# Two gate tiles turned from plain projections into a seven-product pair, and weight loads sorted later, in a planned f32 attention block

## Chip, cores and metric

One core of one Trainium2 chip. The metric is the device time of one execution in microseconds (us), the median of three runs. The kernel is one launch; nothing is computed on the host but constants.

## What is computed

One pre-norm layer on `x` of 512 tokens by 1024 channels, all in f32. One combined projection feeds two attention branches, their SiLU gates and two sigmoid gates. Cut to what matters here:

```
h = rmsnorm(x, norm_g)
(q_lat, c_kv, k_rope, z_a, q_b, k_b, v_b, z_b,
 q_idx, k_idx, w_idx, gate_a, gate_b) = split(h @ w_in)
y_a = mla_attention(...) * silu(z_a)             # 512 wide, dense, chunk-causal
y_b = dsa_attention(..., topk=128) * silu(z_b)   # 512 wide, top-k keys by an indexer
merged = sigmoid(gate_a) * (y_a @ w_o_a) + sigmoid(gate_b) * (y_b @ w_o_b)
out = rmsnorm(x + merged @ w_out, final_g)
```

`gate_a` and `gate_b` are 1024 wide, that is eight tiles of 128 channels each: ga0 to ga7 and gb0 to gb7. `z_b` has four tiles, zb0 to zb3.

## The kernel before, in words

**Arithmetic.** TensorE works in a rounded f32 format, so every operand is split into a high and a low part. The high part is a cast on ScalarE (ACT), the low part a subtraction (`lo_part`, L399, by `tt`, L346) on VectorE (DVE) or GpSimd (POOL). One f32 product is then three matmuls (`mm3`): high by high, high by low, low by high.

**Order.** No loop of the program is the order of the work. Python generators yield steps, and `Flow` (L140 to L258) is a list scheduler that runs at build time: at each turn it takes the step with the smallest key, which is the modelled start time, plus a margin that TensorE (PE) and the DMA queue keep behind other engines (`SETTLE`), plus a small weight of the thread's priority, plus `t.nudge`, a random number below 0.01 us drawn once for each thread from `random.Random(DRAW)`. What comes out is one fixed in-order stream for each engine. All weight loads sit on the DMA queue of SyncE (SP), in order with the other transfers there.

**Weight jobs.** `QUEUE` (L2078) lists the weight tiles. `fetcher` (L953) takes them in that order, gets one of four raw buffers (512 KB each) and issues the load; `splitter` (L967) makes high and low parts; `multiplier` (L980) yields the matmuls, which PE takes between the steps of the attention. A lower-case name is a plain projection (`proj`, L988): 8 blocks of the contraction by 3 matmuls of 128x512, 24 in all, into one PSUM bank. Upper-case names go in twos (`proj2`, L1038): two tiles are one 2x2 block product done by seven products of blocks (`seven`, L1102) instead of eight. Each of the seven is 4 blocks by 3 matmuls of 128x256, 84 for two tiles. For this the weights are summed and subtracted first (`prep`, L1053), seven instead of four pairs of parts are cast and subtracted, and the seven results are put together by two copies on ACT and five 128x256 additions from PSUM on DVE into the slots called `s_pair`. The inputs of the products are sums of blocks of h, `s_hs`; when the last pair has been multiplied, `pair_done` (L1141) gives the `s_hs` slots back and sets "pairs".

**What hangs on "pairs".** `y_gate` (L1690) multiplies the attention result by its SiLU gate, waits for "pairs" (L1698) since its slots `s_ys` are those of `s_hs`, and splits the product: a cast on ACT and one 128x512 scalar_tensor_tensor (STT, L357) on DVE for each of the eight tiles. The first output projection (`branch_out`, L1749; 4 blocks by 3 matmuls of 128x512 with the weights `w_o`) reads `s_ys`. The eight tiles of gate A were moved out to DRAM early (`bias_scratch` serves as that place); when the last projection of all has been emitted ("projections"), `fetch_gates` (L1286) issues their eight loads of 256 KB on SP.

**The tail of the queue.** `ou` takes a load of `w_out` weights, which are only split at that time and multiplied at the end. Before the change the tail is `GB4 GB5 ou zb3 gb6 ou gb7 ou`: one pair, then three plain projections.

**Held loads.** `PASSED` (L2083) holds back the loads of jobs 7 to 10: their DMA is emitted only after 2, 2, 2 and 6 more transfers have been emitted on SP (`hold`, `passed`, L439 to L449). `passed_by` (L1100) does the like for one low part of the values of branch B, which is emitted behind the next addition of a pair.

Of the kernel before, what the change touches and what calls it, by code (L numbers as in the profile page):

```python
# [80 lines left out]
class Step:  # L81
# [58 lines left out]
class Flow:  # L140
# [57 lines left out]
    def run(self, stop=None):  # L198
        while self.threads:
# [15 lines left out]
            for t in self.threads:  # L215
                if isinstance(t.req, Step):
                    for i, (eng, dur, emit) in enumerate(t.req.options):
                        s = self.start(t.req, eng)
                        key = ((self.settled(t.req, eng, s) if eng in SETTLE and s < math.inf else s) + BIAS * t.prio + t.nudge, t.prio)
                        if len(t.req.options) > 1:  # L220
                            fin = s + dur + {"POOL": self.pbias if t.req.pbias is None else t.req.pbias, "ACT": t.req.abias}.get(eng, 0.0)
                            cand = (fin, s, eng, dur, emit, key)
                        else:
                            cand = (0.0, s, eng, dur, emit, key)
                        if i == 0 or cand[0] < mine[0]:
                            mine = cand
                    if best is None or mine[5] < best[1][5]:
                        best = (t, mine)
# [34 lines left out]
NUDGE = 0.01  # L263
DRAW = 53
PSQUARE = -50
# [5 lines left out]
def tile_block(ctx: ExitStack, tc: tile.TileContext, a: dict, out: bass.AP, bias_dram: bass.AP):  # L271
# [166 lines left out]

    held = []  # L439

    def hold(n, emit):

        return lambda: held.append([n, emit])

    def passed():
        for x in list(held):
            x[0] -= 1
            if not x[0]:
                held.remove(x)  # L449
                x[1]()  # L450
# [502 lines left out]
    def fetcher():  # L953
        yield is_done("loads")
        for n, job in enumerate(jobs):
            raw = yield Get(RAW)
            dst = raw[:, : sum(job.widths)]
            if len(job.src.shape) == 3:
                dst = dst.re("p (b c) -> p b c", b=job.src.shape[1])
            step = dma(dst, job.src)  # L960
            if n in PASSED:

                step.options = [("SP", step.options[0][1], hold(PASSED[n], step.options[0][2]))]
            yield step
            job.raw = raw
# [183 lines left out]
    def values2():  # L1149
# [69 lines left out]
        def take(half, out):  # L1219
            v = yield Get(VV)  # L1220
            for u in range(2):
# [3 lines left out]
                yield act(hi, src)  # L1225
                step = lo_part(lo, src, hi)
                if half == 1 and u == 0:

                    step.options = [(e, t, lambda emit=emit: passed_by.append(emit)) for e, t, emit in step.options]
                yield step  # L1230
                put(out[u])
# [936 lines left out]
```

## Time and profile before

| | |
|---|---|
| median of 3 runs | 423.11 us (422.94 to 423.64) |
| the profiled execution's own time | 422.94 us |
| its span in the trace | 421.2 us |
| PE busy | 413.7 us (98%), 2314 matmuls |
| DVE busy | 372.8 us (89%) |
| ACT busy | 265.6 us (63%) |
| POOL busy | 125.2 us (30%) |
| PE in the chain that ended last | 96% |
| mean granted TensorE clock | 0.995 of full speed |

The span is what the trace covers from the first to the last instruction; the execution's own time is 1.74 us longer. A matmul's duration in a row overlaps the next one's, so the pace of PE is read from start to start of groups, or from the matmuls in a stretch without idle time.

### The profile page before, as it was taken

The numbers are of one execution on the slowest core, as the hardware profiler recorded it, in microseconds if no ns is written. First come the engines' busy times: TensorE is split into PE (matmuls) and PEld (weight loads), VectorE is DVE, ScalarE is ACT, GpSimd is POOL, SyncE is SP. The second block draws the span as 40 slices with busy tenths as digits, with TensorE's granted clock in tenths as the row PEclk, the third lists the DMA queues.
The fourth block names the chain that finished last, engine by engine and source line by source line (L and its number), as shares of the span: only waits on it lengthen the run. The fifth ranks groups of instructions, "written<-read, shape, count | busy, mean of one in ns | idle before, by whom it ended". The sixth has DMA issues, their size and how long they took to land.

```text
span 421.2 us, 7078 instructions
## 1 busy us (share of the span) xinstructions
PE 413.7 (98%) x2314; PEld 364.3 (86%) x2314; DVE 372.8 (89%) x797; ACT 265.6 (63%) x596; POOL 125.2 (30%) x139
## 2 busy tenths in 40 slices
PE   8999999999999999999999999999999999999994
PEld 7999878888888888888999988998998888888883
DVE  4879889569999999999999999979799768999995
ACT  5877778586754748625578677694597444336624
POOL 0047768543464669400012000200100000120652
PEclk9999999999999999999999999999999999999998
DMA  7992135665266441444652347144542887248305
GB/s 258 382 337 77 48 94 191 172 206 127 75 156 184 89 151 51 119 146 149 151 163 75 110 142 188 56 166 129 153 138 68 292 296 242 102 148 305 123 1 199
DMA packets 30645, 65.89 MB, mean 156 GB/s; under 512 B 4776, under 2 KB 6200, under 8 KB 30608
## 3 DMA queue, kind: packets, MB, share of 16 engines
q1 hardware_dynamic: 28256, 61.66, 47.4%
q10 hardware_dynamic: 1584, 2.62, 1.7%
q0 software_dynamic: 768, 1.15, 0.9%
q8 instruction: 18, 0.29, 0.3%
q14 instruction: 19, 0.16, 0.1%
HBM read 50.49 MB, written 4.21 MB: 130 GB/s over the span
## 4 chain that ended last, share of the span: by engine, by line
PE 96%; DVE 1%; DMA 1%; issue 0%; POOL 0%; ACT 0%; POOLq 0%; SPq 0%; ACTq 0%
PE ps L418 86%; PE ps L435 5%; PE ps L1583 1%; PE ps L1584 1%; PE ps L1582 1%; PE ps L883 1%; DMA normg<-norm_g 1%; DVE s_xr L357 1%; POOL sm L396 0%; DVE s_rg L357 0%; DVE s_rg L376 0%; ACT s_rg L329 0%; POOLq L2164 0%; ACT s_xg L329 0%; PE ps L932 0%
## 5 line engine op out<-in xcount | busy, mean ns | idle before, releaser
L418 PE MATMUL ps<-s_h,s_w 128*128 128x512 f32 (+1 forms) x732 | 169.9, 379 | 0.0
L418 PEld LDWEIGHTS ps<-s_h,s_w 128*128 128x128 f32 x732 | 128.3, 189 | 22.0
L320 ACT CAST s_w<-raw 128x512 fp32r<-128x512 f32 (+3 forms) x124 | 71.8, 593 | 18.8 <-DMA raw<-w_o 9.3
L348 POOL TENSOR_TENSOR s_w<-raw,s_w 128x512 fp32r<-128x512 f32 (+2 forms) x39 | 48.5, 1255 | 48.1 <-ACT s_w L320 44.2
L346 DVE TENSOR_TENSOR s_w<-raw,s_w 128x512 fp32r<-128x512 f32 (+2 forms) x85 | 55.7, 668 | 4.7 <-ACT s_w L320 3.7
L418 PE MATMUL ps<-s_ys,s_w 128*128 128x512 f32 x192 | 43.8, 389 | 0.0
L418 PEld LDWEIGHTS ps<-s_ys,s_w 128*128 128x128 f32 x192 | 36.0, 188 | 7.5
L329 ACT ACTIVATE s_p<-s_p,sm 128x128 f32<-128x128 f32 (+3 forms) x62 | 32.7, 550 | 5.0 <-DVE sm L1662 4.3
L418 PE MATMUL ps<-s_wo,s_mg 128*128 128x512 f32 (+1 forms) x156 | 33.2, 373 | 0.0
L418 PE MATMUL ps<-s_w,s_xg 128*128 128x328 f32 (+1 forms) x192 | 32.5, 323 | 0.0
L418 PEld LDWEIGHTS ps<-s_wo,s_mg 128*128 128x128 f32 x156 | 27.6, 188 | 5.2
L418 PEld LDWEIGHTS ps<-s_w,s_xg 128*128 128x128 f32 x192 | 31.4, 188 | 0.0
L346 DVE TENSOR_TENSOR s_ph<-ps,s_ph 128x384 fp32r<-128x384 f32 (+1 forms) x48 | 27.6, 593 | 1.0 <-ACT s_ph L320 0.7
L320 ACT CAST s_ph<-ps 128x384 fp32r<-128x384 f32 (+1 forms) x48 | 23.4, 515 | 6.4 <-PE ps L435 5.0
L329 ACT ACTIVATE s_p<-ps,sm 128x128 f32<-128x128 f32 (+3 forms) x32 | 16.8, 527 | 15.7 <-DVE sm L1565 15.6
L348 POOL TENSOR_TENSOR s_p<-s_bias,mask 128x128 f32<-128x128 f32 (+2 forms) x5 | 4.2, 854 | 74.0 <-DMA s_bias<-bias_scratch 39.6
L905 DVE MAX8 sm<-mask 128x8 f32<-128x384 f32 (+2 forms) x48 | 25.7, 549 | 0.2
L906 DVE MATCH_REPLACE8 mask<-sm,mask 128x384 f32<-128x384 f32 (+2 forms) x48 | 25.9, 541 | 0.0
L418 PE MATMUL ps<-s_ph,vv 128*128 128x512 f32 (+3 forms) x128 | 25.1, 318 | 0.0
L435 PE MATMUL ps<-ident,s_p 128*128 128x128 f32 x160 | 23.1, 273 | 0.0
L418 PEld LDWEIGHTS ps<-s_ph,vv 128*128 128x128 f32 x128 | 21.0, 188 | 2.4
L348 POOL TENSOR_TENSOR s_wo<-raw,s_wo 128x512 fp32r<-128x512 f32 x3 | 13.2, 4420 | 28.3 <-ACT s_wo L320 28.3
(194 smaller groups left out, 769.6 us busy)
## 6 DMA issues: line engine op xcount, KB each, us to landing
raw<-w_out SPq DMA_DIRECT2D x18, 512.0 KB, 3.3
s_op<-s_op SPq DMA_DIRECT2D x36, 128.0 KB, 2.3
raw<-w_ga SPq DMA_DIRECT2D x8, 512.0 KB
raw<-w_gb SPq DMA_DIRECT2D x8, 512.0 KB
raw<-w_o SPq DMA_DIRECT2D x16, 256.0 KB, 4.2
s_xn<-x SPq DMA_DIRECT2D x8, 256.0 KB, 4.8
bias_scratch<-s_sig ACTq DMA_DIRECT2D x8, 256.0 KB, 3.0
raw<-w_za SPq DMA_DIRECT2D x4, 512.0 KB, 4.7
```

The costliest lines, as they stand in the source:

```text
L320: nc.scalar.copy(dst.ap, src.ap)
L329: nc.scalar.activation(dst.ap, src.ap, func, **kw)
L346: opts.append(("DVE", 0.07 + 0.00104 * x.n, lambda: nc.vector.tensor_tensor(dst.ap, x.ap, y.ap, op=op)))
L348: opts.append(("POOL", 0.15 + 0.0021 * x.n, lambda: nc.gpsimd.tensor_tensor(dst.ap, x.ap, y.ap, op=op)))
L357: lambda: nc.vector.scalar_tensor_tensor(dst.ap, x.ap, sc(s), y.ap, op0=op0, op1=op1))],
L418: nc.tensor.matmul(ps.ap, l.ap, r.ap, start=start and i == 0, stop=stop and i == len(pairs) - 1, skip_group_check=more)
L435: nc.tensor.transpose(d.ap, s.ap, ident.tile)
L883: yield pe(0.005 + n / 2400, [ps.all], [qs[h].all, ks[0].all], lambda: nc.tensor.matmul(ps.tile[:, :n], qs[h].tile[:96, TOK[i]], ks[0].til ...
L905: yield Step([("DVE", t, lambda: nc.vector.max(m8.tile, work.tile))], [m8], [work])
L906: yield Step([("DVE", t, lambda: nc.vector.match_replace(work.tile, m8.tile, work.tile, MARK))], [work], [m8])
L1582: nc.tensor.matmul(o, q0[0:100], k0[0:100], start=True, stop=False)
L1583: nc.tensor.matmul(o, q0[0:96], k1[0:96], start=False, stop=False)
```

## The change

1. `DRAW` goes from 53 to 27, so every thread's nudge is another number.
2. `PASSED` with `hold` and `passed` is gone. Instead each weight load from the sixth job on (`EARLY_JOBS = 5`) has 2.5 us (`HOLD`) added to its key, so the planner lets other transfers go ahead of it; its modelled start is not changed.
3. `passed_by` is gone; the low part of the values is emitted where it is yielded.
4. The tail of `QUEUE` is `GB4 GB5 GB6 GB7 ou zb3 ou ou`: gb6 and gb7 are a pair, and zb3 is the last projection.

```
             for n, job in enumerate(jobs):
...
             step = dma(dst, job.src)
-            if n in PASSED:
-
-                step.options = [("SP", step.options[0][1], hold(PASSED[n], step.options[0][2]))]
+            if n >= EARLY_JOBS:
+                step.hold = HOLD
             yield step
...
-   key = ((self.settled(...) if ... else s) + BIAS * t.prio + t.nudge, t.prio)
+   key = ((self.settled(...) if ... else s) + t.req.hold + BIAS * t.prio + t.nudge, t.prio)
...
-DRAW = 53
+DRAW = 27
...
         def add(dst, ps, y):
-            step = tt(dst, part(ps), y, ALU.add)
-            return step.then(lambda: [passed_by.pop()() for _ in list(passed_by)])
+            return tt(dst, part(ps), y, ALU.add)
...
-QUEUE = '... sb3 zb2 GB4 GB5 ou zb3 gb6 ou gb7 ou'
+QUEUE = '... sb3 zb2 GB4 GB5 GB6 GB7 ou zb3 ou ou'
...
-PASSED = {7: 2, 8: 2, 9: 2, 10: 6}
+HOLD = 2.5
+EARLY_JOBS = 5
```

On PE, the step from the last projection to the first output projection, before the change. `s_h` is the input h, `s_w` a split weight, `ps` a PSUM bank; the last numbers tell buffers apart. The first four rows are the end of gb7, the others the first w_o product.

```order
L418 MATMUL ps_93<-s_h_628,s_w_3980 128x512
L418 MATMUL ps_93<-s_h_653,s_w_3979 128x512
L418 MATMUL ps_93<-s_h_654,s_w_3979 128x512
L418 MATMUL ps_93<-s_h_653,s_w_3980 128x512
L418 MATMUL ps_99<-s_ys_3866,s_w_4003 128x512
L418 MATMUL ps_99<-s_ys_3874,s_w_4003 128x512
L418 MATMUL ps_99<-s_ys_3866,s_w_4004 128x512
```

And with the change: the end of the last of the seven products of gb6 and gb7 (the rows with `s_hs`), then the first rows of zb3.

```order
L419 MATMUL ps_92<-s_hs_2267,s_w_3933 128x256
L419 MATMUL ps_92<-s_hs_2266,s_w_3934 128x256
L419 MATMUL ps_92<-s_hs_2338,s_w_3933 128x256
L419 MATMUL ps_92<-s_hs_2339,s_w_3933 128x256
L419 MATMUL ps_92<-s_hs_2338,s_w_3934 128x256
L419 MATMUL ps_95<-s_h_593,s_w_3982 128x512
L419 MATMUL ps_95<-s_h_594,s_w_3982 128x512
L419 MATMUL ps_95<-s_h_593,s_w_3983 128x512
```

Before, 72 matmuls of three plain projections (and some of the attention) lie between the last product of a pair and the first w_o product; with the change zb3's 24 do, and directly behind them stand `ps_94<-s_ys_4057,s_w_4038`, `ps_94<-s_ys_4064,s_w_4038` and `ps_94<-s_ys_4057,s_w_4039`.

On DVE, the splits of the gated results before the change: among the last attention products' low parts (`s_ph`), from the row after the last sum of the pair (`s_pair`).

```order
L346 TENSOR_TENSOR s_pair_3678<-ps_96,s_pair_3678 128x256
L346 TENSOR_TENSOR s_ph_3766<-ps_97,s_ph_3761 128x384
L357 SCALAR_TENSOR_TENSOR s_ys_3880<-s_y_3517,s_ys_3872 128x512
L346 TENSOR_TENSOR s_ph_3758<-ps_93,s_ph_3757 128x512
L357 SCALAR_TENSOR_TENSOR s_ys_3879<-s_y_3236,s_ys_3871 128x512
L346 TENSOR_TENSOR s_ph_3789<-ps_99,s_ph_3788 128x512
L357 SCALAR_TENSOR_TENSOR s_ys_3876<-s_y_1969,s_ys_3868 128x512
```

With the change they stand behind all of the attention: `s_y_3946<-ps_98,s_tmp_3998` is the last attention result, and these sixteen rows run from it to the low part of the first w_o weight, `s_w_4039`, which is the row after them (five are shown in words: `s_y_3946`, a sum on ps_92, `s_w_4010`, `s_wo_4023` and a sum on ps_99 come first).

```order
L347 TENSOR_TENSOR s_wo_4034<-raw_67,s_wo_4033 128x512
L347 TENSOR_TENSOR s_wsum_4024<-raw_69 128x512
L347 TENSOR_TENSOR s_pair_3863<-ps_92,s_pair_3863 128x256
L358 SCALAR_TENSOR_TENSOR s_ys_4067<-s_y_2220,s_ys_4060 128x512
L358 SCALAR_TENSOR_TENSOR s_ys_4069<-s_y_3222,s_ys_4062 128x512
L358 SCALAR_TENSOR_TENSOR s_ys_4066<-s_y_1969,s_ys_4059 128x512
L358 SCALAR_TENSOR_TENSOR s_ys_4068<-s_y_2965,s_ys_4061 128x512
L358 SCALAR_TENSOR_TENSOR s_ys_4065<-s_y_1669,s_ys_4058 128x512
L358 SCALAR_TENSOR_TENSOR s_ys_4064<-s_y_1436,s_ys_4057 128x512
L358 SCALAR_TENSOR_TENSOR s_ys_4070<-s_y_3533,s_ys_4063 128x512
L347 TENSOR_TENSOR s_wo_4044<-s_wsum_4024,s_wo_4043 128x512
L347 TENSOR_TENSOR s_w_4039<-raw_66,s_w_4038 128x512
```

All seven splits moved behind the last sum of the second pair, and one `w_out` part stands between them and `s_w_4039`.

On SP, the loads around the eight gate tiles (`s_sig<-bias_scratch`) before the change:

```order
L458 DMA raw_66<-w_o 128x512
L458 DMA raw_67<-w_out 128x2x512
L458 DMA raw_69<-w_o 128x512
L458 DMA raw_68<-w_o 128x512
L458 DMA raw_66<-w_out 128x2x512
L458 DMA raw_67<-w_o 128x512
L458 DMA raw_69<-w_o 128x512
L458 DMA s_sig_4089<-bias_scratch 128x512
```

and with it:

```order
L446 DMA raw_66<-w_o 128x512
L446 DMA raw_68<-w_out 128x2x512
L446 DMA raw_67<-w_o 128x512
L446 DMA raw_69<-w_o 128x512
L446 DMA s_sig_4117<-bias_scratch 128x512
L446 DMA s_sig_4119<-bias_scratch 128x512
```

Five w_o loads stood ahead of the eight gate loads, now three do; a `w_out` load and the fourth w_o load follow behind the eight in both.

## Rows read from the trace of the kernel before

**Rows 1.** Part 1 of the page: busy time, share of the span and number of instructions of each engine.

```profile
span 421.2 us, 7078 instructions
PE 413.7 (98%) x2314; PEld 364.3 (86%) x2314; DVE 372.8 (89%) x797; ACT 265.6 (63%) x596; POOL 125.2 (30%) x139
```

**Rows 2.** Part 4 of the page: the chain of work that ended last, by engine.

```profile
PE 96%; DVE 1%; DMA 1%; issue 0%; POOL 0%; ACT 0%; POOLq 0%; SPq 0%; ACTq 0%
```

**Rows 3.** The waits view for PE: line waited on, releaser, us in total, times, longest.

```profile
PE ps L541 <- DVE neghalf L492: 1.1, 1, 1.1
```

**Rows 4.** Groups of instructions on PE by form: line, engine, operation, out<-in, shape, type, count, then busy us, mean ns of one, idle before.

```profile
L418 PE MATMUL ps<-s_h,s_w 128*128 128x512 f32 x624 | 155.1, 395 | 0.0
L418 PE MATMUL ps<-s_hs,s_w 128*128 128x256 f32 x144 | 19.8, 285 | 0.0
L418 PE MATMUL ps<-s_h,s_w 128*128 128x256 f32 x108 | 15.0, 283 | 0.0
```

**Rows 5.** PE's timeline from 306 us to the first w_o product: start us, length us, engine, line, operation, count (a row is a run of like instructions).

```profile
306.94 1.95 PE L418 MATMUL ps<-s_hs,s_w 128*128 128x256 f32 x15
308.72 1.60 PE L418 MATMUL ps<-s_h,s_w 128*128 128x256 f32 x12
310.17 0.82 PE L435 MATMUL ps<-ident,s_p 128*128 128x128 f32 x6
310.74 1.68 PE L418 MATMUL ps<-s_hs,s_w 128*128 128x256 f32 x12
312.25 0.60 PE L435 MATMUL ps<-ident,s_p 128*128 128x128 f32 x4
...
324.12 0.57 PE L418 MATMUL ps<-s_ph,vv 128*128 128x256 f32 x4
324.52 8.38 PE L418 MATMUL ps<-s_h,s_w 128*128 128x512 f32 x36
332.75 3.56 PE L418 MATMUL ps<-s_ys,s_w 128*128 128x512 f32 x15
```

**Rows 6.** Two links of the chain that ended last, in order of time: start us, length us, engine, line, count; both are stretches of 256-column products.

```profile
223.69 5.75 PE ps L418 x48
229.87 4.77 PE ps L418 x38
```

**Rows 7.** DVE's timeline from 307 to 329 us, columns as in rows 5, with idle time before a row and its releaser in brackets.

```profile
307.77 0.42 DVE L346 TENSOR_TENSOR s_pair<-ps,s_pair 128x256 f32<-128x256 f32 x1
308.10 0.74 DVE L376 TENSOR_SCALAR s_p<-s_p,sm 128x256 f32<-128x256 f32 x2
...
316.01 3.09 DVE L357 SCALAR_TENSOR_TENSOR s_ys<-s_y,s_ys 128x512 fp32r<-128x512 f32 x5
319.02 0.55 DVE L346 TENSOR_TENSOR s_ph<-ps,s_ph 128x384 fp32r<-128x384 f32 x1
...
321.15 0.67 DVE L346 TENSOR_TENSOR s_w<-raw,s_w 128x512 fp32r<-128x512 f32 x1
321.75 0.67 DVE L346 TENSOR_TENSOR s_wo<-raw,s_wo 128x512 fp32r<-128x512 f32 x1
322.35 0.67 DVE L346 TENSOR_TENSOR s_w<-raw,s_w 128x512 fp32r<-128x512 f32 x1
...
325.45 0.69 DVE L346 TENSOR_TENSOR s_y<-ps,s_tmp 64x512 f32<-64x512 f32 x1
326.15 0.69 DVE L357 SCALAR_TENSOR_TENSOR s_z<-s_z,ps 128x512 f32<-128x512 f32 x1
...
328.65 0.69 DVE L357 SCALAR_TENSOR_TENSOR s_ys<-s_y,s_ys 128x512 fp32r<-128x512 f32 x1 [0.48 <-ACT s_ys L329]
```

**Rows 8.** ACT's timeline, rows of 314 to 341 us, columns as in rows 7.

```profile
314.79 2.21 ACT L329 ACTIVATE s_ys<-s_y 128x512 fp32r<-128x512 f32 x4
...
324.73 0.58 ACT L320 COPY s_tmp<-ps 64x512 f32<-64x512 f32 x1 [0.45 <-PE ps L418]
...
341.10 0.62 ACT L320 CAST s_w<-raw 128x512 fp32r<-128x512 f32 x1 [6.98 <-DMA raw<-w_o]
```

**Rows 9.** The DMA queue of SP on the timeline, 323 to 342 us: start us and length us of the issues.

```profile
323.65 0.80 SPq L458 DMA_DIRECT2D raw<-w_o  x2
324.86 0.38 SPq L458 DMA_DIRECT2D raw<-w_out  x1
328.20 2.11 SPq L458 DMA_DIRECT2D raw<-w_o  x2
330.36 3.74 SPq L458 DMA_DIRECT2D s_sig<-bias_scratch  x8
334.20 0.38 SPq L458 DMA_DIRECT2D raw<-w_out  x1
334.68 6.79 SPq L458 DMA_DIRECT2D raw<-w_o  x4
```

**Rows 10.** Windows: busy us and count of PE, PEld, DVE, ACT and POOL in a stretch, granted clock, share of the DMA engines, GB/s.

```profile
306.00:316.00 10.00, 10.00 (x73) 9.36 (x72) 9.30 (x25) 10.00 (x25) 0.00 (x0) 1.00 0.36 132
333.00:341.00 8.00, 8.00 (x37) 6.64 (x36) 3.39 (x6) 1.11 (x2) 0.00 (x0) 1.00 0.99 370
360.00:380.00 20.00, 20.00 (x90) 16.57 (x89) 20.00 (x39) 8.22 (x15) 4.25 (x3) 1.00 0.35 121
```

**Rows 11.** Part 6 of the page: DMA issues, KB each, median us from issue to landing.

```profile
raw<-w_o SPq DMA_DIRECT2D x16, 256.0 KB, 4.2
```

More of the change, by code (lines that the diff above doesn't have):

```diff
@@ L87 @@
     pair = False
+    hold = 0.0
     pbias = None
@@ L218, in run @@
                         s = self.start(t.req, eng)
-                        key = ((self.settled(t.req, eng, s) if eng in SETTLE and s < math.inf else s) + BIAS * t.prio + t.nudge, t.prio)
+                        key = ((self.settled(t.req, eng, s) if eng in SETTLE and s < math.inf else s) + t.req.hold + BIAS * t.prio + t.nudge, t.prio)
                         if len(t.req.options) > 1:
@@ L437, in turn @@
         return pe(0.107 * len(parts), [d for d, _ in parts], [s for _, s in parts] + [ident.all], emit, len(parts))
[L439 to L450, printed above, removed]
     def dma(dst, src):
@@ L457, in dma @@
             n *= x
-        return Step([("SP", n / 360000.0, lambda: (nc.sync.dma_start(d, s), passed()))], bufs(dst), bufs(src))
+        return Step([("SP", n / 360000.0, lambda: nc.sync.dma_start(d, s))], bufs(dst), bufs(src))
     def pool_dma(dst, src):
@@ L1098, in proj2 @@
         Job(a[second[0]][second[1]], [512, 512], body, prep=prep)
-    passed_by = []
     def seven(times, part, c11, c21, c12, c22, end):
@@ L1225, in take @@
                 yield act(hi, src)
[L1226 to L1230, printed above, removed]
+                yield lo_part(lo, src, hi)
                 put(out[u])
@@ L2077 @@
 ORDER = [0,1,2,3]
-QUEUE = 'ga0 ga1 pe ma0 va0 ga2 za0 ma1 va1 ga3 za1 ma2 ga4 za2 ma3 ga5 za3 sb0 zb0 ga6 ga7 sb1 VB GB0 GB1 sb2 zb1 GB2 GB3 sb3 zb2 GB4 GB5 ou zb3 gb6 ou gb7 ou'
+QUEUE = 'ga0 ga1 pe ma0 va0 ga2 za0 ma1 va1 ga3 za1 ma2 ga4 za2 ma3 ga5 za3 sb0 zb0 ga6 ga7 sb1 VB GB0 GB1 sb2 zb1 GB2 GB3 sb3 zb2 GB4 GB5 GB6 GB7 ou zb3 ou ou'
 LATE = 0.5
```

## The prediction

> **What bounds the kernel now.** I first read the busy times [rows 1]: PE works 413.7 us of a span of 421.2, so at most 7.5 us are not matmuls. The chain that ended last is PE for 96% [rows 2], and the waits view for PE has a single line of 1.1 us, at the very start [rows 3]. So the time is the sum of the matmuls at their pace, plus head and tail, and every other engine only matters where it makes PE wait. DVE is the one that can: over the span it is busy for 372.8 us [rows 1], between 306 and 316 us for 9.3 of 10 us, and between 360 and 380 for all of it [rows 10]. PE is still never stopped there. An edit can gain by fewer or shorter matmuls alone, and lose by a new wait or by a slower pace.
>
> **The sum, matmuls.** Two plain projections were 2 x 24 matmuls of 512 columns; the pair is 84 of 256 columns. The time per matmul has to be a pace, not a mean length (395 and 285 ns in [rows 4]), since lengths overlap. For 512 columns the best row is the one in which gb7 itself runs: 36 matmuls from 324.52 to 332.75 [rows 5], 8.23 / 36 = 0.2286 us. So 48 cost 10.97 us. For 256 columns, from start to start [rows 5]: 15 in 1.78 us (0.119), 12 in 1.45 (0.121), 12 in 1.51 (0.126); in the long stretch [rows 6] 48 in 5.75 (0.120). I take 0.120: 84 cost 10.08 us. PE gains 10.97 - 10.08 = **0.9 us**. The gain is this small because an eighth of the columns goes away, but 256 columns cost 0.120 where half of 0.2286 would be 0.114. The ends: at 0.126 for the small ones the gain is 0.4; with the pace of the w_o stretch for the large ones (37 in 8.0 us, 0.216 [rows 10]) it is 10.4 - 10.1 = 0.3; at 0.119 it is 1.0. I take 0.85, since the 0.2286 is the row of the very work that is removed.
>
> A page rule speaks against the change. The Trainium skill, page "TensorE: Matmul & The Clock Gate", section "Back-to-back issue gap", says that weight load and matmul together set the spacing in a stream of pairs, with 131 ns sustained for 512 columns and 81 ns for 128; an estimate between the two for 256 columns is 98 ns, and by it 48 x 0.131 - 84 x 0.098 = -1.9 us, a loss, which with the wait below would end at 425.5 us. This trace does not have that pace: its 512-column row is at 0.2286 us, far over 0.131. The same section's gap for an isolated matmul (216 and 109 ns) is near the rows and would make the gain 1.2 us.
>
> **The sum, other engines.** One pair more brings three casts and two copies more on ACT, seven results to put together and four sums of weights. DVE has 16 rows more in its stream (748 to 764), among them five 128x256 additions from PSUM, whose pace is 0.33 us (307.77 to 308.10 [rows 7]); the rest are 512-wide at 0.60 us (321.15, 321.75, 322.35 [rows 7]) or smaller, since some choices also went from POOL to DVE. That is about 7 us of DVE work. Most of it is hidden at nothing, by DVE's 421.2 - 372.8 = 48 us of idle time and PE's uncovered streams of matmuls; where that cover is thin is the next step. The dropped hold of jobs 7 to 10, the 2.5 us and the new nudges permute the streams; I cost them at nothing, since PE's work in between is the same and no load was waited for by PE [rows 3]; the price if not is a rival.
>
> **The sum, the new wait.** Before, the splits of the gated results (s_ys) run on DVE from 313.61 on, since the last pair ended at about 312.3 (the row at 310.74 [rows 5]); five of them are the row at 316.01 [rows 7], and PE first wants one at 332.75 [rows 5], over 13 us later. With the change they stand behind the last sum of the new pair, and PE has only zb3 in between. I set t = 0 at the start of the PE group behind the last attention product; in before that is 324.52.
>
> PE from there: 9 + 12 + 12 matmuls of the pair's last three products, 33 x 0.120 = 3.96 us, and zb3's 24 x 0.2286 = 5.49. So the first w_o matmul is due at 9.45, and its third, which reads the low weight s_w_4039, at 9.45 + 2 x 0.2286 = 9.9.
>
> DVE from there: the last attention result is copied by ACT (324.73, 0.58 long [rows 8]) and added by DVE at 325.45 [rows 7], so at t = 0.93. From this addition up to s_w_4039 the stream has 16 rows, all dependent on DVE's order: 13 of 512 columns at 0.60 (seven of them s_ys) and 3 of 256 at 0.33, 7.80 + 0.99 = 8.79. The low weight then starts at 9.72 and ends 0.68 later, at 10.4; about 0.15 more until PE sees it (ACT's copy ended at 325.31 and DVE's addition started at 325.45 [rows 7, 8]): 10.55. **PE waits 10.55 - 9.9 = 0.65 us** in the first w_o product. The s_ys rows themselves are in time: the one for block 0 ends at 8.6. From below: at 0.126 for the 33 small matmuls PE comes 0.2 later, and with a DVE row of 0.58 (five s_ys in 3.09 with the overlap, 0.602 [rows 7]) nothing is gained, so 0.3 is about the least with this order. From above: the w_o load lands 4.2 us after its issue [rows 11], and that issue waits for a raw buffer which DVE frees only just before t = 0. The cast on ACT ahead of the seven s_ys casts could then start at 4.0 instead of 2.4, and seven casts of 0.53 (four in 2.21 [rows 8]) follow; that adds up to 0.5, so 1.2.
>
> Behind this wait on PE is the whole w_o stretch, and nothing later catches it up, as PE is the bound to the end. The sum is -0.85 + 0.65 = -0.2 us against the profiled execution's 422.94 us (0.17 under the median of 423.11): **422.7 us**.
>
> **Rivals.**
>
> 1. *No new wait.* If DVE has no backlog at t = 0 and a split row or two fall into PE's favour (POOL or an earlier position does part of it), PE goes straight through and the whole 0.85 to 1.2 stays: 421.75 to 422.1. For it: DVE had idle time around 328 [rows 7]. Against: the 16 rows are in order behind the last attention result, and none may pass.
>
> 2. *The gate loads push back the fourth w_o tile* (the slower end). Eight loads of 256 KB take SP 3.74 us to issue and DMA runs at 370 GB/s with a 0.99 share [rows 9, 10]. In before a w_o tile behind them landed at 341.10, 10.7 us after their first issue at 330.36, and ACT had waited 6.98 us for it [rows 8, 9]; PE wanted that tile (the sixth) at 332.75 + 5 x 2.72 = 346.4. With the change only three w_o tiles stand ahead. The first gate load goes out at about t = 4.75 (behind the freeing of a raw buffer by row `s_wsum_4024`), so the fourth tile lands at 15.5, its parts are there at 16.7, and PE wants it at 10.1 + 3 x 2.74 = 18.3. The slack is 1.6 us. It decides if the eight loads start or the tile lands over 1.6 us later than this; the fourth tile's own issue stands behind a w_out load that waits for s_w_4039, so that is possible. At 2 us late beyond the slack's end: 422.7 + 1.3 to 2.1 = 424.0 to 424.8.
>
> 3. *The new order opens a wait elsewhere.* Where the attention's softmax and sums are on DVE and PE's cover of weight products is thin, one or two more 0.60 us rows from POOL, with their latency, give 1 to 2 us: 423.7 to 424.7. Against: before 306 us PE never waited [rows 3], though DVE was as full.
>
> 4. *The small matmuls are no cheaper.* If the weight load rather than the columns sets the pace, 84 small ones cost as much as 48 large ones from 10.97 / 84 = 0.131 us on; at 0.14 it is 0.8 more instead of 0.85 less, 424.4. No 256-column row is over 0.126 [rows 5, 6]. The sustained pace that the Trainium skill gives would lead here as well.
>
> **How the numbers follow.** My forecast, a small gain with a wait at the first w_o product, has 0.48 (its own range 422.1 to 423.3); rival 1 has 0.24, rival 2 0.13, rival 3 0.12, rival 4 0.03. A measurement tells 0.2% from no change, 0.85 us on the median: under 422.26 is faster, over 423.96 slower. Faster: nearly all of rival 1 and the forecast's lower end, 0.23 + 0.06 = 0.29. Slower: 0.10 of rival 2, 0.07 of rival 3, 0.02 of rival 4, 0.19. The same: 0.52. The range of 8 in 10 goes from rival 1's middle, 421.8, to the lower half of rivals 2 and 3, 424.3.
>
> **What would show it.** PE would have 36 matmuls more, 2350, and a busy time about 0.9 lower without idle; the waits view for PE would have a second line, at a w_o product, waiting for DVE's s_w or s_ys, of 0.3 to 1.2 us; DVE's row of seven s_ys would end less than 2 us before PE's first s_ys row, and start only after the last s_pair row. I am wrong if that line is missing (rival 1), if a line waits for ACT's or DVE's parts of the fourth w_o tile, with ACT waiting for the DMA (rival 2), if the lines lie before 300 us (rival 3), or if the 256-column groups have a pace over 0.13 (rival 4).

## The result, and the profile after

The changed kernel takes 427.57 us (median of four, 426.58 to 430.69), the kernel before beside it 423.38 (422.94 to 423.77): a ratio of 1.0113, 95% interval 1.0078 to 1.0149. It is slower by some 4 us; the forecast was 422.7, and the range ended at 424.3. The profiled executions differ by 3.64 us: 426.58 against 422.94 us, spans of 424.8 and 421.2. All times below are medians of the fast executions, without one of e1 (514.02 us, granted clock 0.752) and one of e10 (2354.74 us).

Part 1 of the page of the kernel after, to be held against [rows 1]:

```profile
span 424.8 us, 7170 instructions
PE 414.8 (98%) x2350; PEld 365.4 (86%) x2350; DVE 384.7 (91%) x813; ACT 266.8 (63%) x597; POOL 115.5 (27%) x139
```

PE has its 36 matmuls more, DVE 11.9 us of work more, and POOL 9.7 us less. PE's busy time rose by 1.1 us, where the prediction expected it to fall by 0.9; e1 below, which has the pair's gain of 0.89 us, shows 415.3, so the sum of matmul lengths did not measure that gain. The chain that ended last has changed far more than the busy times [rows 2]:

```profile
PE 61%; DVE 19%; DMA 11%; ACT 4%; issue 3%; SPq 1%; POOL 0%; POOLq 0%; DVEq 0%; ACTq 0%
```

The waits view for PE, which had one line [rows 3], now has four:

```profile
PE ps L529 <- DVE neghalf L480: 1.1, 1, 1.1
PE ps L1562 <- DMA s_op<-kpeh: 0.8, 1, 0.8
PE ps L1563 <- DMA s_op<-kpel: 0.3, 1, 0.3
PE ps L419 <- DVE s_w L347: 0.3, 1, 0.3
```

The last line is the wait that the prediction put at the first w_o product. The two in the middle nobody expected. PE's timeline at both places (columns as in rows 5):

```profile
84.80 0.86 PE L419 MATMUL ps<-s_h,s_w 128*128 128x512 f32 x3
85.50 0.85 PE L419 MATMUL ps<-s_lat,s_w 128*128 128x512 f32 x3
87.20 0.33 PE L1562 MATMUL ps<-s_op,qhi 100*128 100x128 f32 x1 [0.85 <-DMA s_op<-kpeh]
87.85 0.33 PE L1563 MATMUL ps<-s_op,qhi 96*128 96x128 f32 x1 [0.32 <-DMA s_op<-kpel]
...
325.27 1.29 PE L419 MATMUL ps<-s_hs,s_w 128*128 128x256 f32 x9
...
329.27 5.63 PE L419 MATMUL ps<-s_h,s_w 128*128 128x512 f32 x24
334.74 0.61 PE L419 MATMUL ps<-s_ys,s_w 128*128 128x512 f32 x2
335.64 1.66 PE L419 MATMUL ps<-s_ys,s_w 128*128 128x512 f32 x6 [0.28 <-DVE s_w L347]
```

Where the first logits of branch A read the copied keys (`s_op`), PE stands still for most of 86.35 to 87.85 us. Then the queue of SP around it, first the kernel after and then the kernel before (columns as in rows 9):

```profile
78.86 0.54 SPq L446 DMA_DIRECT2D raw<-w_ga  x1
79.44 1.18 SPq L446 DMA_DIRECT2D s_qs<-s_th  x2
80.73 0.52 SPq L446 DMA_DIRECT2D raw<-w_za  x1
81.34 0.85 SPq L446 DMA_DIRECT2D s_op<-kpeh  x1
82.30 0.58 SPq L446 DMA_DIRECT2D s_op<-kpel  x1
```

```profile
74.20 0.52 SPq L458 DMA_DIRECT2D raw<-w_ga  x1
...
79.96 0.86 SPq L458 DMA_DIRECT2D s_op<-kpeh  x1
80.87 0.57 SPq L458 DMA_DIRECT2D s_qs<-s_th  x1
81.55 0.52 SPq L458 DMA_DIRECT2D s_op<-kpel  x1
...
83.54 0.53 SPq L458 DMA_DIRECT2D raw<-w_za  x1
```

Before, za1's load of 512 KB went out behind the copies of the keys, and ga3's nearly 6 us ahead of them. Now both stand right ahead, and the copy issued at 82.30 takes 5.5 us (a link of the chain). The copies' own issue is only 0.7 to 1.4 us later.

DVE's timeline at the first w_o product and at the end:

```profile
329.76 0.41 DVE L347 TENSOR_TENSOR s_pair<-ps,s_pair 128x256 f32<-128x256 f32 x1
330.09 4.28 DVE L358 SCALAR_TENSOR_TENSOR s_ys<-s_y,s_ys 128x512 fp32r<-128x512 f32 x7
334.31 0.67 DVE L347 TENSOR_TENSOR s_wo<-s_wsum,s_wo 128x512 fp32r<-128x512 f32 x1
334.91 0.68 DVE L347 TENSOR_TENSOR s_w<-raw,s_w 128x512 fp32r<-128x512 f32 x1
...
400.61 1.37 DVE L347 TENSOR_TENSOR s_wo<-raw,s_wo 128x512 fp32r<-128x512 f32 x1 [0.82 <-ACT s_wo L321]
401.90 1.79 DVE L347 TENSOR_TENSOR s_wo<-s_wsum,s_wo 128x512 fp32r<-128x512 f32 x1
...
412.16 1.27 DVE L358 SCALAR_TENSOR_TENSOR s_xr<-ps,s_xr 128x512 f32<-128x512 f32 x2
```

and the row of before that answers to the last:

```profile
408.63 1.38 DVE L357 SCALAR_TENSOR_TENSOR s_xr<-ps,s_xr 128x512 f32<-128x512 f32 x2 [0.98 <-PE ps L418]
```

Before, DVE waited here for PE's results: it was ahead. After, it comes without a wait: PE's results lie ready and DVE is behind. Part of that lies in the two rows at 400.61 and 401.90, which took 1.37 and 1.79 us, while a row of 128x512 takes 0.60 elsewhere (six `s_xr` rows in 3.69 us at 406.01). POOL subtracts at the same time, in rows of 1.30 and 1.45 us; before, the two late subtractions of POOL took 11.46 us together, beside rows of DVE that were not slowed (two `s_wo` in 1.29 us at 397.20). After, then before:

```profile
400.13 1.30 POOL L349 TENSOR_TENSOR s_wo<-raw,s_wo 128x512 fp32r<-128x512 f32 x1 [3.39 <-ACT s_wo L321]
401.70 1.45 POOL L349 TENSOR_TENSOR s_wo<-raw,s_wo 128x512 fp32r<-128x512 f32 x1 [0.27 <-ACT s_wo L321]
```

```profile
394.81 11.46 POOL L348 TENSOR_TENSOR s_wo<-raw,s_wo 128x512 fp32r<-128x512 f32 x2
```

The two long rows hold DVE for 3.0 us (400.61 to 403.61) instead of 1.2. That is 1.8 us more, and the end comes only 1.02 us later behind PE than before (table below).

How full DVE is shows in the windows of 332 to 418 us (columns as in rows 10), before, after, the pair alone on the old order (e1, below), and all of the change but the pair (e3, below):

```profile
332.00:418.00 86.00, 82.91 (x389) 69.31 (x387) 74.73 (x138) 39.61 (x79) 20.17 (x10) 0.99 0.53 185
```

```profile
332.00:418.00 86.00, 85.21 (x397) 70.90 (x395) 82.51 (x145) 41.28 (x82) 9.66 (x9) 1.00 0.54 184
```

```profile
332.00:418.00 86.00, 83.31 (x382) 68.19 (x381) 80.98 (x142) 39.10 (x78) 11.00 (x8) 1.00 0.53 180
```

```profile
332.00:418.00 86.00, 86.00 (x402) 71.94 (x400) 76.82 (x134) 38.93 (x76) 17.18 (x11) 1.00 0.53 182
```

DVE's idle time in these 86 us falls from 11.3 to 3.5 us with the change, and to 9.2 us without the pair.

**Where the 3.6 us lie.** I cut each profiled execution at PE rows that all kernels have (the first row of each kind), and took from each stretch its matmuls at one price for each width: 0.2286 us for 512 columns and 0.120 for 256 [rows 5, 6], 0.172, 0.148, 0.145 and 0.058 for 384, 328, 320 and 128, 0.095 for a transpose. What is left is the loss. The absolute values carry the error of the prices, but the prices are the same in every row, so differences between rows count. "Start" is how much later than before PE reaches 27 us (its first row `ident,rstd`). us:

| | start | to `s_latraw` | to `s_ph,vv` | to `s_hs` | to `s_ys` | to `s_wo` | to PE's end | behind PE | span |
|---|---|---|---|---|---|---|---|---|---|
| before | 0.00 | 0.21 | 1.91 | 3.06 | 2.78 | -0.35 | -0.06 | 6.29 | 421.2 |
| after | 0.08 | 0.37 | 4.29 | 3.16 | 2.94 | 0.24 | -0.06 | 7.31 | 424.8 |
| e1 pair alone | 0.88 | 0.20 | 1.93 | 3.06 | 2.78 | 0.73 | 2.96 | 6.29 | 425.3 |
| e2 draw alone | 0.17 | 0.21 | 2.81 | 3.26 | 5.68 | -0.32 | -0.08 | 6.49 | 425.6 |
| e3 after without pair | 0.27 | 0.32 | 4.36 | 3.16 | 2.96 | -0.32 | -0.09 | 6.98 | 425.0 |
| e5 holds alone | -0.13 | 0.79 | 1.96 | 3.05 | 3.59 | -0.32 | -0.08 | 7.67 | 423.9 |
| e8 one load held | 0.87 | 0.20 | 2.67 | 3.21 | 2.94 | 0.26 | -0.03 | 8.21 | 424.8 |
| e9 e8, fewer sums | 0.38 | 0.20 | 2.70 | 3.16 | 2.94 | 0.28 | -0.06 | 6.43 | 422.5 |
| e10 e1, gates later | 0.64 | 0.20 | 1.93 | 3.06 | 2.79 | -0.37 | 3.89 | 6.29 | 424.9 |
| e16 before, fewer sums | 0.11 | 0.23 | 1.91 | 3.06 | 2.80 | -0.35 | -0.05 | 6.23 | 421.3 |

After minus before: 2.38 us up to the first `s_ph,vv` (the keys), 0.59 in the w_o stretch, 1.02 behind PE's last matmul, 0.50 in small pieces elsewhere, and 0.89 less matmul work: 3.60. The start differs by up to 0.9 us between kernels whose streams are the same there (before, e1, e10 and e16: 0.00, 0.88, 0.64 and 0.11), so it belongs to the execution and not to the edit.

Against e3, which lacks only the pair, the change shows what the pair does in the new order: 0.89 less matmul work, 0.56 more in the w_o stretch, 0.33 more behind PE, in sum nothing. The forecast for the pair was -0.2; the medians of the two (427.57 and 426.77) lie within each other's scatter. What lies between before and e3 is the order's: 3.8 us of span, 3.4 in the medians.

### The profile page after: what moved, and what is told of

Same layout as the page of the kernel before. It is cut to its first block, busy times and chain, and to the rows that moved or that the text cites. A ratio compares the mean times of both kernels' runs of the same rounds, so it can differ in the third digit from the quotient of the medians.

```text
span 424.8 us, 7170 instructions
## 1 busy us (share of the span) xinstructions
PE 414.8 (98%) x2350; PEld 365.4 (86%) x2350; DVE 384.7 (91%) x813; ACT 266.8 (63%) x597; POOL 115.5 (27%) x139
## 4 chain that ended last, share of the span: by engine, by line
PE 61%; DVE 19%; DMA 11%; ACT 4%; issue 3%; SPq 1%; POOL 0%; POOLq 0%; DVEq 0%; ACTq 0%
PE ps L419 52%; PE ps L436 4%; DMA raw<-w_out 3%; DMA s_x<-xT 3%; DVE s_wo L347 2%; DVE s_mg L347 2%; DVE s_tmp L358 2%; DVE s_wsum L347 2%; DVE s_pair L347 2%; DMA raw<-w_o 1%; DVE s_w L347 1%; DMA s_op<-kpel 1%; PE ps L1563 1%; DMA s_xn<-x 1%; PE ps L1564 1%
## 5 line engine op out<-in xcount | busy, mean ns | idle before, releaser
L419 PE MATMUL ps<-s_h,s_w 128*128 128x512 f32 (+1 forms) x720 | 164.6, 373 | 0.1
L419 PEld LDWEIGHTS ps<-s_h,s_w 128*128 128x128 f32 x720 | 123.6, 189 | 20.4 <-DVE s_op L358 0.3
L321 ACT CAST s_w<-raw 128x512 fp32r<-128x512 f32 (+3 forms) x126 | 72.8, 594 | 11.6 <-DVE raw L347 5.2
L347 DVE TENSOR_TENSOR s_w<-raw,s_w 128x512 fp32r<-128x512 f32 (+2 forms) x87 | 57.1, 671 | 4.1 <-ACT s_w L321 3.9
L330 ACT ACTIVATE s_p<-s_p,sm 128x384 f32<-128x384 f32 (+3 forms) x58 | 31.1, 560 | 5.1 <-DVE sm L1642 5.0
L321 ACT CAST s_ph<-ps 128x384 fp32r<-128x384 f32 (+1 forms) x48 | 23.3, 514 | 10.4 <-PE ps L436 9.6
L419 PE MATMUL ps<-s_ph,vv 128*128 128x512 f32 (+3 forms) x128 | 26.2, 320 | 0.0
L419 PE MATMUL ps<-s_hs,s_w 128*128 128x256 f32 x192 | 26.1, 284 | 0.0
L893 DVE MAX8 sm<-mask 128x8 f32<-128x256 f32 (+2 forms) x48 | 25.5, 547 | 0.5 <-POOL mask L480 0.2
L894 DVE MATCH_REPLACE8 mask<-sm,mask 128x256 f32<-128x256 f32 (+2 forms) x48 | 25.8, 540 | 0.0
L419 PEld LDWEIGHTS ps<-s_hs,s_w 128*128 128x128 f32 x192 | 24.5, 191 | 0.3
```

Of the source, the lines that this page charges most:

```text
L321: nc.scalar.copy(dst.ap, src.ap)
L330: nc.scalar.activation(dst.ap, src.ap, func, **kw)
L347: opts.append(("DVE", 0.07 + 0.00104 * x.n, lambda: nc.vector.tensor_tensor(dst.ap, x.ap, y.ap, op=op)))
L419: nc.tensor.matmul(ps.ap, l.ap, r.ap, start=start and i == 0, stop=stop and i == len(pairs) - 1, skip_group_check=more)
L893: yield Step([("DVE", t, lambda: nc.vector.max(m8.tile, work.tile))], [m8], [work])
L894: yield Step([("DVE", t, lambda: nc.vector.match_replace(work.tile, m8.tile, work.tile, MARK))], [work], [m8])
```

## The experiments

All were timed beside the kernel before. Each ratio is to it, with its 95% interval.

**The parts of the change, each by itself.** e1 is the kernel before with the new queue, e2 with the new draw; e3 is the kernel after with the old queue.

```
-QUEUE = '... GB4 GB5 ou zb3 gb6 ou gb7 ou'
+QUEUE = '... GB4 GB5 GB6 GB7 ou zb3 ou ou'
```

> The kernel before with the new tail of QUEUE alone (gb6 and gb7 a pair); old draw, loads held as before, so SP's stream is the old one up to some 300 us. Theory A (the loss is made before 110 us, by two weight loads that now stand ahead of the small key copies on SP): the pair is innocent, time 422.3 to 423.6, that is 0.9 of gain less the 0.3 us wait at the first w_o product, plus up to 0.5 of DVE backlog at the end. Theory B (the pair makes the loss, by DVE's backlog from 330 us to the end): 425.5 to 427.5, with DVE the last link at the end. Theory C (the new nudges): as the kernel before less 0.6, 422.3 to 423.

```
-DRAW = 53
+DRAW = 27
```

> The kernel before with DRAW 27 alone. Here ga3's load stays ahead and za1's stands between the last two key copies. Theory A: 423 to 424.5, since one 512 KB load stands ahead of one key copy. Theory B: 423 to 423.8, no change. Theory C (any other draw costs this much): 426 to 427.5.

```
-QUEUE = '... GB4 GB5 GB6 GB7 ou zb3 ou ou'
+QUEUE = '... GB4 GB5 ou zb3 gb6 ou gb7 ou'
```

> The changed kernel with the old tail of QUEUE, so all of the change but the pair. Theory A: 426.5 to 428.5, the loss stays, with PE waiting for the key copies at about 86 us. Theory B: 422.9 to 423.8. Theory C: 426 to 427.5, without that wait being what costs it.

Measured: e1 428.07 us (ratio 1.0112, 1.0085 to 1.0138), e2 427.45 (1.0126, 1.0077 to 1.0175), e3 426.77 (1.0084, 1.0058 to 1.011). The queue alone and the draw alone each cost as much as all together: the parts do not add up. (The third part, the holds, is e5 below.) e1 lies above all its ranges, e2 fits theory C, e3 theories A and C. In e1 PE's stream is that of before up to the pair. Its start is late by 0.88, its first `s_hs` row stands at 207.85 against 206.96, and its first `s_ys` row at 332.75 in both: the pair gives 0.89 us. It is lost again behind that:

```profile
341.60 35.94 PE L418 MATMUL ps<-s_ys,s_w 128*128 128x512 f32 x156 [0.52 <-ACT s_w L320]
...
411.23 0.50 PE L418 MATMUL ps<-s_wo,s_mg 128*128 128x512 f32 x1 [1.94 <-ACT s_wo L320]
411.96 1.42 PE L418 MATMUL ps<-s_wo,s_mg 128*128 128x512 f32 x5 [0.22 <-DVE s_wo L346]
```

The 0.52 is rival 2 (ACT's cast of the fourth w_o tile had waited 3.88 us for its load). In e2 0.9 us is lost around the keys without a wait of PE; most of the loss is elsewhere, two waits in the middle of the kernel:

```profile
225.18 3.02 PE L418 MATMUL ps<-s_w,s_h 128*128 128x256 f32 x23 [1.13 <-DVE s_w L346]
...
233.85 1.46 PE L418 MATMUL ps<-s_hs,s_w 128*128 128x256 f32 x10 [1.10 <-DVE s_w L346]
```

e3 loses 2.4 us in the stretch of the keys, like the kernel after: that loss is the order's, not the pair's.

**Other orders.** e5 is the kernel after with the old draw and the old queue, so parts 2 and 3 of the change (the 2.5 us, and no `PASSED` or `passed_by`) alone; e6 is the kernel after with the old draw; e7 is the kernel before with one more draw.

```
-DRAW = 27
+DRAW = 53
...
-QUEUE = '... GB4 GB5 GB6 GB7 ou zb3 ou ou'
+QUEUE = '... GB4 GB5 ou zb3 gb6 ou gb7 ou'
```

> The kernel before with the 2.5 us and without PASSED and passed_by: old draw, old tail. Theory D (PE never waits in the one order of before; every other order of the same work loses 3 to 5 us, in several places): 425.5 to 428. Theory E (the loss belongs to the 2.5 us, which leave two loads ahead of the key copies): 426 to 427.5, with 2 us or more lost before 110 us, as in the changed kernel. Theory F (draw 27 is what loses): 423 to 424.3.

```
-DRAW = 27
+DRAW = 53
```

> The changed kernel with the old draw, 53. Theory D: 425.5 to 428. Theory E: 426 to 427.5, with the early loss. Theory F: 422.5 to 424, since the pair gains 0.9.

```
-DRAW = 53
+DRAW = 1
```

> The kernel before with DRAW 1, nothing else. Theory D: 425.5 to 428, losing in places of its own. Theories E and F: 423 to 424.5.

Measured: e5 425.08 (1.0037, 1.0016 to 1.0057), e6 429.98 (1.0146, 1.0105 to 1.0188), e7 430.49 (1.0153, 1.0129 to 1.0176). Three orders, three losses, each at another place: e5 behind PE's end (7.67 instead of 6.29) and, by the table, 0.6 us before 45 us and 0.8 in the middle, e6 in several waits, most of them for parts of w_o and w_out, e7 in one wait of 4.3 us for ACT's `s_wo` at 402. Two redraws (27 and 1) cost 1.3 and 1.5%. None of the three times lies in a range of its theories, and theory E is refuted: e5 and e6 have the 2.5 us without `PASSED`, and lose nothing around the keys (e5 1.96 against 1.91 in the table). In both, za1's load still goes out behind the last copy; in e5:

```profile
82.46 0.52 SPq L446 DMA_DIRECT2D s_op<-kpel  x1
83.08 0.53 SPq L446 DMA_DIRECT2D raw<-w_za  x1
```

With draw 27 and the old holds (e2), it goes out at 84.08, between the last two copies. So neither the new holds nor the new draw alone puts it ahead of all four; the two together do (after and e3).

**The keys' copies.** e8 is the kernel after with za1's load held back until four more transfers have been issued, so behind the four copies; e4 holds ga3's load too.

```
+PASSED = {10: 4}
...
+            if n in PASSED:
+                step.options = [("SP", step.options[0][1], hold(PASSED[n], step.options[0][2]))]
```

> The changed kernel with one load, za1's, issued behind the four key copies; ga3's stays ahead of them (the step that e4 undid for both). If the key copies wait for the bytes ahead of them: the wait at the first logits falls from 1.2 us to 0.3 to 0.8 us, no wait for weights of ga3 comes in its place, and the time is 0.5 to 1.2 under the changed kernel's, 426.4 to 427. Theory D alone: no change beyond 0.3.

```
-PASSED = {10: 4}
+PASSED = {9: 6, 10: 5}
```

> The changed kernel with two loads, of ga3 and za1, held back on SP until the four key copies of the first two heads have been issued; the streams of the other engines are unchanged. Theory A: PE's wait at the first logits (1.2 us in two rows) is gone and the time falls by 1.2 to 3 us, to 424 to 426, and the runs lie closer together. Theory B: no change, 426.5 to 428. Theory C: no change, or a later wait for the two weights of under 1 us.

Measured: e8 426.24 (1.0059, 1.0041 to 1.0076), e4 427.33 (1.0092, 1.0077 to 1.0107). e8 gains 1.3 us on the changed kernel, a little more than forecast; e4 gains nothing beyond the scatter, where theory A wanted 1.2 to 3. In e8 the copies are issued as late as in the changed kernel (81.33 to 83.75), the first logits have no wait, and the stretch loses 1.6 us less:

```profile
86.12 0.86 PE L419 MATMUL ps<-s_lat,s_w 128*128 128x512 f32 x3
86.81 0.23 PE L1578 MATMUL ps<-s_op,qhi 100*128 100x128 f32 x1
```

So it is the big load ahead on the queue that delays the small copies: 1.6 of the 2.38 us. The other 0.8 stays in e8 and e9, and e2 has 0.9; these are kernels with draw 27. Those with draw 53 and the 2.5 us (e5, e6) don't have it, so it goes with the order that this draw makes; by what step stays open. The Trainium skill, page "DMA: Bandwidth & Descriptors", section "Queues, rings and completion order", says that each DMA engine takes a queue's descriptors in ring order; the 5.5 us of a 64 KB copy behind two 512 KB loads agree. e4 brings other waits for that (0.5 and 0.3 us for ACT's `s_p`) and keeps 4.11 of loss there, by the same reckoning. And e8's span is still 424.8: its execution started 0.79 later, so its PE ends 0.9 us earlier than after's, but DVE's row at 400.61 stands at 400.60, and 8.21 us follow PE's end. Something behind PE takes the gain. The chain that ended last shows a part of it. In both kernels the row at 400.6 hangs on the last w_out load, whose raw buffer DVE had freed; in the kernel after (start us, length us):

```profile
393.19 6.21 DMA raw<-w_out
```

In e8 that link is 393.52, 5.88 long. Both end at 399.40, and then ACT's cast and DVE's long row follow.

**DVE's amount of work.** e9 is e8 without four of six late sums into `s_xr`, 4 x 0.60 us; e16 the kernel before, e17 is e10 (below) with the same edit.

```
-                yield soon(tt(r, r, u, ALU.add, BOTH))
+                if half == 0:
+                    yield soon(tt(r, r, u, ALU.add, BOTH))
```

> The kernel of e8 (one load held) without four of the six late sums s_xr<-s_xr,s_part, so the part of the output that they bring is left out; PE's stream is the same, and DVE has some 1.8 us less to do near 406 us (three 512-wide rows net, since one s_wo part comes from POOL to DVE). Theory G (from the pair on the end is set by DVE, not by PE): the span falls by 1.2 to 1.9 us from e8's 424.8, and the time from 426.24 to 424.4 to 425.1. Rival (PE still sets the end): no change, 426 to 426.6.

> Control for e9: the kernel before without the same four of six sums into s_xr (that part of the output is left out). If DVE's amount of work sets the end only with the new order, while PE does before: 422.8 to 423.4, a ratio of 0.9985 to 1.000, and PE stays over 93% of the chain. Rival, that these sums cost the end in any order, so that e9 says nothing on the change: 421.3 to 422.1, a ratio of 0.995 to 0.997.

> e10 (the pair on the old order with the gate loads later) without the same four sums. If DVE's amount of work is what its last 0.9 us wait and its end hang on: 1.0 to 2.5 under e10's 428.38, that is 425.9 to 427.4, and the wait for DVE's s_wo near 398 us under 0.3. Rival, that it is only the place of one DVE row in the order: 428.0 to 428.8 and the wait stays at 0.8 to 1.0.

Measured: e9 424.29 (1.0017, 1.0004 to 1.0029), 1.95 under e8, and DVE is ahead of PE again at the end:

```profile
409.79 1.38 DVE L358 SCALAR_TENSOR_TENSOR s_xr<-ps,s_xr 128x512 f32<-128x512 f32 x2 [0.66 <-PE ps L419]
```

e16 423.48 (1.0002, 0.9992 to 1.0011): in the kernel before the same sums cost nothing. e17 424.32 (1.0025, 1.001 to 1.004), 4.0 under e10, more than the 2.4 us of work left out. So the time of DVE's rows sets the end with the new order, and does not before. How much of that is the number of rows and how much the two long ones beside POOL, these runs don't separate: e9 has one of 1.60 us (400.06) and not two, since a part moved from POOL to DVE. e9 lies just under its range, e16 just over. e17 shows the same direction for the pair on the old order; both numbers of its expectation missed: the gain is larger, and its profiled execution, the longest of its ten at 426.44 us, still has a wait of 1.94 us for `s_wo`, so the profile doesn't show where the others gained.

**The gate loads and the squares, on e1.** e10 issues six of the eight gate loads later, e11 moreover gives ACT's late squares no preference.

```
+GATES = {2: 2, 3: 3, 4: 6, 5: 7, 6: 9, 7: 10}
...
+            if c in GATES:
+                step.options = [("SP", step.options[0][1], hold(GATES[c], step.options[0][2]))]
```

> The kernel of e1 (pair alone) with six of the eight gate loads issued behind two to six of the w_o and w_out loads that follow them; nothing else moves. If the loads push back the fourth w_o tile (rival 2 of the prediction): PE's wait of 0.5 us at its first matmul is gone and the loss between the first w_o and the first output product falls from 1.1 to under 0.5 us. The time falls by as much only if DVE is not the bound behind it: Theory G gives 0 to 0.3 of time, the rival 0.5 to 0.8 (428 from 428.76).

```
-PSQUARE = -50
+PSQUARE = 0
```

> The kernel of e10 with PSQUARE 0 in place of -50: the last w_out cast on ACT now stands ahead of the squares that wait for DVE, and one of the late parts is on POOL. PE's 1.9 us wait at the end of e1 (for an ACT part that stood behind those squares) should be gone: 1.0 to 2.2 us less than e10 if that wait is what the end hangs on; under Theory G in its strict form 0 to 0.6 less, since DVE is behind by itself.

Measured: e10 428.32 (1.0116, 1.0094 to 1.0138), e11 426.7 (1.0077, 1.0055 to 1.01). e10 removes rival 2's wait (the `s_ys` row runs through, 192 matmuls from 332.52), and gets another for it:

```profile
397.75 11.15 PE L418 MATMUL ps<-s_wo,s_mg 128*128 128x512 f32 x59 [0.93 <-DVE s_wo L346]
410.84 0.50 PE L418 MATMUL ps<-s_wo,s_mg 128*128 128x512 f32 x1 [1.94 <-ACT s_wo L320]
411.56 1.42 PE L418 MATMUL ps<-s_wo,s_mg 128*128 128x512 f32 x5 [0.22 <-DVE s_wo L346]
```

e11 turns both into one of 3.31 us for DVE's `s_wo`. Its time fell by 1.6 us from e10's, within the range for "the end hangs on ACT's wait"; its profiled execution (427.30 us) is one of its longer ones and e10's (426.64) the shortest, so their rows don't show where the 1.6 us lie. e10's time is e1's (428.07) within the scatter, though rival 2's wait is gone. Waits taken away one by one come back at the next w_out part. That they have one cause, DVE being late, is argued and not shown: e10's second wait comes through a cast of ACT (410.19) that stands behind squares which had waited 9.2 us for DVE's `s_xr`, and between its two waits DVE has two long rows (1.78 us each) beside POOL.

**Work given to POOL.** Low parts of w_out for the seventh product (and in e13 and e15 its differences) go to POOL: e12 on e1, e13 on e10, e14 on e8, e15 on e14.

```
-        yield soon(lo_part(lo.all, raw, hi.all))
+        yield soon(lo_part(lo.all, raw, hi.all, ("POOL",) if key[0] == 7 else BOTH))
```

> The kernel of e1 (pair alone) with the four low parts of the w_out differences (product 7) forced onto POOL, where they were on DVE; PE's order is unchanged. DVE has 2.4 us less to do between 316 and 360 us. Theory G: the waits of PE for s_wo at the end shrink, 1 to 2.5 us less than e1, 426.3 to 427.8. Rival (the loss hangs on single transfers or on ACT's order, not on DVE's amount of work): within 0.5 of e1, 428.3 to 429.3.

> The kernel of e8 (the changed kernel with one load held) with the four low parts on POOL. One of them stood on DVE right ahead of the low part that PE waited for at the first w_o product, so that wait of 0.3 us should be gone. Theory G: the end, set by DVE, comes 1.5 to 2.4 us earlier, until PE's own end plus 6.3 us of tail holds it: 424 to 425 from 426.24. Rival: 425.8 to 426.6.

```
-   yield soon(tt(t.all.f, raw[1], raw[0], ALU.subtract, BOTH))
+   yield soon(tt(t.all.f, raw[1], raw[0], ALU.subtract, ("POOL",) if product == 7 else BOTH))
```

> The kernel of e10 (pair, gate loads later) with these four low parts and the four differences themselves on POOL: DVE has 4.8 us less to do behind 316 us. Theory G: back to the time of the kernel before or under it by up to the pair's 0.9, 422.5 to 424.5. Rival: a new wait for POOL's slower sums (1.7 us and more each, raw buffers held longer) keeps it at 425 to 428.

> The kernel of e14 with the four differences on POOL as well. Theory G: no better than e14 by more than 0.5, since PE sets the end by then: 423.8 to 425. Rival: POOL's sums hold the raw buffers longer and it is slower than e14 by 0.5 to 2.

Measured: e12 428.24 (1.0104, 1.008 to 1.0128), e13 431.61 (1.0178, 1.0148 to 1.0207), e14 427.14 (1.0078, 1.0047 to 1.011), e15 428.96 (1.0114, 1.0087 to 1.0141). None is better than its base; e12 and e15 agree with their rivals, e13 and e14 are slower than both ranges. In e14 a POOL part takes 1.3 to 2.6 us where DVE takes 0.60, and the first w_o wait grew from 0.28 to 1.56 us, since another order on DVE came with it (`s_w` now at 334.50, behind a row that waits 1.19 us for ACT's `s_z`). The Trainium skill, page "GPSIMD Engine Reference", section "4.1 Engine selection", puts two-input elementwise work at some twice DVE's time there; 1.30 against 0.60 agrees. Why other parts take 1.79 and 2.60 is open: at 342.82 a part of 1.30 stands beside a DVE that is busy all the time, where DVE's own row is the long one (1.20 at 343.46). Since every such edit also redraws the order, these four don't tell whether DVE's amount or POOL's lateness decided; only that this way out does not work.

## Why the prediction was wrong

- **The matmuls: right.** 0.85 to 0.9 us were forecast, e1 shows 0.89, and after's groups have the widths and the means expected [rows 4]. The 33 small matmuls from 325.27 to 329.27 have a pace of 0.121 us, so rival 4 is out:

```profile
L419 PE MATMUL ps<-s_h,s_w 128*128 128x512 f32 x576 | 145.2, 396 | 0.1
L419 PE MATMUL ps<-s_hs,s_w 128*128 128x256 f32 x192 | 26.1, 284 | 0.0
```

- **The new wait: right in place and mechanism, near in size.** From t = 0 at 325.27, the first w_o row is at 9.47 (forecast 9.45), the low weight starts at 9.64 (9.72) and ends at 10.32 (10.4), PE goes on at 10.37 (10.55). The wait is 0.28 as the trace counts idle time, a little under the range of 0.3 to 1.2, and 0.59 by the table, in it; 0.65 was forecast.
- **The step that failed: "The dropped hold of jobs 7 to 10, the 2.5 us and the new nudges permute the streams; I cost them at nothing, since PE's work in between is the same and no load was waited for by PE".** It cost 2.38 us around the keys, and 3.4 us in all (e3 against before), where the sum had nothing. That no load was waited for held for the old order, in which za1's load stood behind the copies; it is no evidence for another order. I had looked at SP's stream around 330 us, where the queue's tail changes, and not at jobs 7 to 10, which the diff names. e3 shows the loss without the pair, and e8 gives 1.6 us of it back. Of the three things that the step names, none does it alone: e5 has the new holds and e2 the new nudges, and in neither does PE wait for the keys. The other 0.8 us goes with the new draw, stands in no wait of PE, and stays open. This is rival 3 in its heading only, at a place that it had ruled out, at more than its price of 1 to 2 us, and by a queue instead of DVE's rows.
- **The second: "Most of it is hidden at nothing, by DVE's 421.2 - 372.8 = 48 us of idle time".** Of these 48 us, 22.5 lie before 100 us and only 11.3 behind 332, where 7.8 us of work came on top (in all 11.9, not 7, since more work went over from POOL, whose time fell by 9.7). DVE is late at the end, by 1.02 us behind PE. e9 and e16 show that this sets the time: the same four sums are worth 1.95 us with the new order and nothing in the old. But the pair's added work is only part of it: e3 has no pair, 9.2 us of idle time left in the stretch, and is still late by 0.69 us, and e5 by 1.38. The pair adds 0.33. So the term was put at nothing too easily, but idle time, even in the right stretch, doesn't measure it. What counts is when DVE's last rows come, and there the two rows beside POOL (1.8 us over their usual time) are a rival that no run here removes by itself.
- **Rival 2** is not in the kernel after: ACT waited 1.18 us for the fourth w_o tile's load, and PE for nothing. In e1 it is there, at 0.52 us.

So with all of the change PE's 0.89 us is paid away: after and e3 have spans of 424.8 and 425.0, with and without the pair. On e1's order the pair costs more, since 3.0 us are lost to w_out's parts at the end. I cannot say which single row of DVE made the last difference there.

## What to carry to other kernels

When a change permutes in-order streams, price the permutation, and look first at the small transfers that big ones may now precede: a stream without waits is evidence for the order that it has, not for another one. An engine's idle time over the span, or even near the end, doesn't say that added work is free; find the row that the end hangs on and when it comes. In this stream two new draws alone cost 1.3 and 1.5%, so an edit must be tried both with its own order and with the old, and be worth more than that.

## What was unexpected of the hardware

Subtractions of 128x512 at the same time on DVE and POOL make rows of one of the two long: 1.37 and 1.79 us instead of 0.60 on DVE in the kernel after, 11.46 us for two instead of 1.30 each on POOL in the kernel before. In all traces here together, 61 rows of DVE with two inputs of 128x512 behind 332 us took over 0.9 us, and all 61 overlap a row of POOL. So moving such a row from one to the other does not free the first for all of the row's time.

A wait of PE can also cost more than its length, when the granted clock falls behind it. e17's profiled execution, PE's row and the windows behind it:

```profile
398.68 14.07 PE L418 MATMUL ps<-s_wo,s_mg 128*128 128x512 f32 x65 [1.94 <-DVE s_wo L346]
```

```profile
396.00:399.00 3.00, 1.06 (x5) 0.57 (x4) 2.84 (x6) 2.32 (x6) 3.00 (x2) 1.00 0.55 213
399.00:402.00 3.00, 3.00 (x10) 2.37 (x9) 3.00 (x4) 1.66 (x3) 0.77 (x1) 0.55 0.01 3
402.00:404.00 2.00, 2.00 (x13) 1.87 (x13) 2.00 (x5) 0.00 (x0) 0.00 (x0) 0.83 0.00 0
```

The clock is at 0.55 for the next three us, near its lower level of 1.2 GHz. The 65 matmuls from the wait to the last product take 13.90 us (398.68 to 412.58); in e10, whose clock stayed at 1.00 there, the same 65 take 12.91 without the two waits among them. e11 shows it too (0.60 from 400 to 404 us, behind its wait of 3.31 us); behind the waits of 1.94 us at the end of e1 and e10 the clock stayed at 1.00. In the profile of the kernel after it is 1.00 from 332 to 418 us, but its longest execution (430.69 us) has a mean of 0.991 where the other three have 0.996 or 0.997 and 426.58 to 427.75. That may be why the changed kernels scatter more than the kernel before; no trace of such an execution of the kernel after shows it.
